# Attention opened on the in-projection's side of SBUF, beside the recurrence's last chunks

## The chip, the cores and the metric

The kernel runs on one core of a Trainium2 chip. The metric is the device time of one execution in microseconds (us). Engines: PE (TensorE matmul, with PEld its weight loads), DVE (VectorE), ACT (ScalarE), POOL (GpSimd), SP (SyncE, here the queue that issues nearly all DMAs).

## What is computed

One decoder layer over 1024 tokens of width 1024, all in float32. Cut to what matters here:

```python
h = _rmsnorm(x, mix_norm_gain)
proj = h @ w_in                                  # 1024 x 3232
p_rwkv, p_attn = proj[..., :1696], proj[..., 1696:]
y_rwkv = _rwkv7_mixer(p_rwkv, ...)               # 8 heads x 64, a recurrence over the tokens
q, k, v = split(p_attn, 3)                       # 8 heads x 64
q, k = _partial_rotary(q), _partial_rotary(k)    # first 16 of 64 dims
o = _rmsnorm(_dilated_attention(q, k, v))        # causal, three (window, dilation) patterns merged
x = x + concat([y_rwkv, o]) @ w_out
h = _rmsnorm(x); gate, val = split(h @ w_ffn_up, 2)      # 2 x 2816
x = x + (silu(_causal_dwconv(gate)) * val) @ w_ffn_down
return _rmsnorm(x)
```

## The kernel before

**A planner fixes the order.** Every step is recorded as an operation with a duration per engine that may run it, a rank (lower goes first), the operations that it waits for and the buffers that it uses. `Plan.run(until)` is a list scheduler in Python, run while the kernel is built. It takes in turn the operation that can start first by those durations, the lower rank winning, issues it, and stops once all of `until` are issued. So it writes one fixed instruction order per engine; on the chip every engine and the SP queue go through theirs strictly in order. The planner only knows waits on data and on its own rings of buffers. Where a pool is opened on the memory of a closed one, the tile framework adds waits on the chip: with `reuse_waits="tile"` the first use of a new tile waits for the last use of what lay there. SBUF and PSUM are two-ended stacks: a pool lies on the left end or, with `side="right"`, on the right end.

**The stages**, in order of time:
- The norm of x and the RWKV columns of the in-projection, with the preparation of the recurrence (prep pools, left).
- The recurrence: 16 chunks of 64 tokens in 8 units (`unit(q)`, two chunks each), pools `rp`, `pch` (the banks `pzu`, `pzs`) and `pxt` on the left, `rf` (its output side) on the right. A chunk is a chain PE L941, L950, ACT copy, PE L963, ACT copy, PE L973, L1016, DVE L989, DVE and POOL L994, to the next chunk's L941. A unit needs first a triangular solve on DVE (L869, L875), a round trip through DRAM, and two groups of small matmuls (PE L906, L912). When both chunks are done, its output is normed and stored (`yrw_d`).
- Beside it, at the lowest rank (200 + j), the twelve attention columns of the in-projection, `attn_in(j)`: 128 columns of q, k or v each, 48 matmuls of 512 columns (L456 to L458, tile `pb_at`), each half then stored to `qkv_d`. They read hT_hi and hT_lo (64 KB of each partition) and weight tiles on the right. Columns 0 to 10 may run as soon as PE has room. **Column 11 is held back** by `chain["Y"]`, the last copy of the last chunk. The rotary step (`rotated`) reloads q and k columns, turns them and stores them.
- `attention()`: per head, q and k are loaded and split in a high and a low part (ACT or DVE cast L267/L269, POOL subtractions L1149 and L1153), v is transposed (PE L1160), then for 8 blocks of queries scores (PE L1188, L1189), mask and maximum (DVE L1192), exponential (ACT L1202), transposes (PE L1220) that are split again (L1231), weighted sums (PE L1250), and two closing steps per head. Its pools (some 90 KB) are opened on the **left, over the recurrence's**, so after `left.close()`.
- The out-projection: part 0 (`y_rwkv`; PE L1383 to L1385, 192 matmuls, rank 301 and up) needs only the recurrence's output and runs beside the attention at a lower rank; part 1 needs the attention heads. Then the second norm, the FFN's up side, and its down side.

The order of these openings is written out at the end of the layer:

```python
plan.run([*rotated, *mixed_out[:-1], chain["Y"]])
left.close()
attention()
plan.run([*mixed_out, *(o for os_ in cols_out.values() for o in os_)])
right.close()
```

**PSUM** has 8 banks. Short-lived results of all stages share one ring named "t", slots in strict rotation: 4 in the recurrence (`ps` x2, `pxt` x2), 5 in the attention (`ps` x2, `pxa` x3). A slot's next user waits for its last one. `pin` (2 banks, right) belongs to the in-projection, `pzu` and `pzs` to the recurrence, `pa` (1) to the attention, `pacc` (2) to the out-projection.

Of the kernel before, what the change touches and what calls it, by code (L numbers as in the profile page):

```python
# [15 lines left out]
PSUM = bass.MemoryType.PSUM  # L16
# [53 lines left out]
class Buf:  # L70


    def __init__(self, ring, make):
        self.ring, self.make, self.t, self.ops = ring, make, None, []

    def free_at(self):
        return None if any(o.end is None for o in self.ops) else max(o.end for o in self.ops)


class Plan:  # L80
# [70 lines left out]
    def run(self, until=None):  # L151

        until = list(until) if until is not None else None
        while any(self.todo.values()):
# [3 lines left out]
            for eng, ops in self.todo.items():  # L158
# [5 lines left out]
                s, i = got[0]  # L164
# [9 lines left out]
            for b in o.bufs:  # L174
                if b.t is None:
                    b.t = b.make()
                    self.used[b.ring].append(b)
# [24 lines left out]
def planned_layer(ctx: ExitStack, tc: tile.TileContext, a, out):  # L202
# [10 lines left out]
    plan = Plan()  # L213
# [18 lines left out]
    turns = []  # L232

    def t_ring(*pools):
        turns[:] = pools
        plan.ring("t", len(pools))
        plan.banks.add("t")

    def t_new(name):
        def make():  # L240
            pool, tag = turns[len(plan.used["t"]) % len(turns)]
            return pool.tile([P, 512], F32, tag=tag, name=name)

        return plan.buf("t", make)
# [463 lines left out]
    def attn_in(j, after=None):  # L708
        R = 200 + j

        def evacuate(n, acc, m, d):
            spl = spl_n(f"spl{j}_{n}")

            def put(eng):
                if j >= 4:
                    copy(eng, spl.t, acc.t)
                else:
                    scaled(eng, spl.t, acc.t, 0.125)

# [353 lines left out]
    cols_out[11] = attn_in(11, chain["Y"])  # L1073
# [44 lines left out]
    def attention():  # L1118
        pa = att.enter_context(tc.tile_pool(name="pa", bufs=1, space=PSUM, reuse_waits="tile"))
        pxa = att.enter_context(tc.tile_pool(name="pxa", bufs=3, space=PSUM, reuse_waits="tile"))  # L1120
        ap_ = att.enter_context(tc.tile_pool(name="ap", bufs=1, reuse_waits="tile"))
        t_ring((ps, "t"), (pxa, "x"), (pxa, "x"), (ps, "t"), (pxa, "x"))
# [12 lines left out]
        def head_operands(h, R):  # L1135
# [3 lines left out]
            qin = [load(qd, lambda b=b: qd.t[b : b + 64], lambda: heads[h], 0.73, R) for b in (0, 64)]  # L1139
# [3 lines left out]
                    cols_out[8 + h // 2] if b else (),  # L1143
# [619 lines left out]
    xpool = outp.enter_context(tc.tile_pool(name="xpool", bufs=1, side="right", reuse_waits="tile"))  # L1763
    wop = outp.enter_context(tc.tile_pool(name="wop", bufs=1, side="right", reuse_waits="tile"))
    wop0 = wop0_.enter_context(tc.tile_pool(name="wop0", bufs=1, side="right", reuse_waits="tile"))
# [4 lines left out]
    low, up_left, up_right, at = ExitStack(), ExitStack(), ExitStack(), {}  # L1770
    at["low"] = low.enter_context(tc.tile_pool(name="rawp", bufs=1, reuse_waits="tile"))
    pup = up_left.enter_context(tc.tile_pool(name="pup", bufs=1, space=PSUM, reuse_waits="tile"))
    hp2 = up_left.enter_context(tc.tile_pool(name="hp2", bufs=1, reuse_waits="tile"))
    tmpn_ = ExitStack()
    pxn = tmpn_.enter_context(tc.tile_pool(name="pxn", bufs=2, space=PSUM, reuse_waits="tile"))
    tmpn = tmpn_.enter_context(tc.tile_pool(name="tmpn", bufs=1, reuse_waits="tile"))
# [14 lines left out]
    dlow = dlow_.enter_context(tc.tile_pool(name="dlow", bufs=1, side="right", reuse_waits="tile"))  # L1791
    at["ps1"] = up_right.enter_context(tc.tile_pool(name="ps1", bufs=1, space=PSUM, side="right", reuse_waits="tile"))
    at["late"] = up_right.enter_context(tc.tile_pool(name="late", bufs=1, side="right", reuse_waits="tile"))
# [5 lines left out]
    at["last"] = up_right.enter_context(tc.tile_pool(name="last", bufs=1, side="right", reuse_waits="tile"))  # L1799
    at["ps2"] = up_right.enter_context(tc.tile_pool(name="ps2", bufs=1, space=PSUM, side="right", reuse_waits="tile"))  # L1800
# [5 lines left out]
    up_right.close()  # L1806
    up_left.close()
    dn_ = ExitStack()
    pdn = dn_.enter_context(tc.tile_pool(name="pdn", bufs=6, space=PSUM, reuse_waits="tile"))
    dp = dn_.enter_context(tc.tile_pool(name="dp", bufs=1, side="right", reuse_waits="tile"))  # L1810
# [83 lines left out]
```

## Time and profile before

| | |
|---|---|
| median of 3 runs | 1441.2 us (1432.59 to 1442.34) |
| profiled execution: its own time, its span | 1448.17 us, 1446.0 us |
| PE busy over the span | 1378.2 us (95%) |
| DVE, ACT, POOL busy | 999.4, 555.0, 334.1 us |
| mean granted TensorE clock | 0.979 of full |

The rows below are times from the span's start. In the views of stretches each engine has its busy time and its count of instructions; PEclk is the mean granted clock, 1.00 standing for 2.4 GHz and 0.50 for 1.2 GHz; then the share of the 16 DMA engines and GB/s. In a timeline the columns are start, duration, engine, line, operation, output<-inputs, shapes, count, and in brackets the idle time just before and what ended it.

### The profile page before, as it was taken

What the parts mean: (1) busy time and instruction counts of PE and PEld (TensorE: products, weight loads), DVE (VectorE), ACT (ScalarE), POOL (GpSimd) and SP (SyncE); (2) the same over time, 40 slices, a digit from 0 to 9 for tenths busy, and PEclk for the clock granted to TensorE, in tenths of its full rate; (3) what the DMA queues carried; (4) which work ended last, traced back from release to release, by engine and by line L of the source; (5) the groups of instructions that cost most, each with busy time, mean ns of one, the idle gap of its engine ahead of it and who ended that gap; (6) DMA issues with size and microseconds to landing.
All of it is one profiled execution on the core that took longest, in us unless ns stands there. A gap on an engine that the chain in (4) does not pass through costs nothing.

```text
span 1446.0 us, 21020 instructions
## 1 busy us (share of the span) xinstructions
PE 1378.2 (95%) x7872; PEld 1137.7 (79%) x7872; DVE 999.4 (69%) x2018; ACT 555.0 (38%) x961; POOL 334.1 (23%) x364
## 2 busy tenths in 40 slices
PE   5999999999999889999889999999999998999997
PEld 4788887788777778898767888888888876888886
DVE  5566663878777279897678867677776757565556
ACT  5432332133332268775344434433333434122113
POOL 4223223144443367642211000000000004111101
PEclk9999999999999899999989999999999999999999
DMA  6143348545653365432633322222222228322203
GB/s 180 44 145 119 129 140 253 147 138 138 175 146 88 87 200 151 131 114 88 220 131 98 88 87 74 72 87 82 79 87 88 69 79 288 123 97 88 88 29 117
DMA packets 172564, 173.02 MB, mean 120 GB/s; under 512 B 39632, under 2 KB 142416, under 8 KB 171440
## 3 DMA queue, kind: packets, MB, share of 16 engines
q1 hardware_dynamic: 172320, 171.16, 38.9%
q8 instruction: 62, 1.02, 0.3%
q10 hardware_dynamic: 144, 0.52, 0.1%
q14 instruction: 38, 0.31, 0.1%
HBM read 119.22 MB, written 52.43 MB: 119 GB/s over the span
## 4 chain that ended last, share of the span: by engine, by line
PE 53%; DVE 4%; DMA 2%; issue 1%; ACT 1%; POOL 1%; SPq 0%; DVEq 0%; POOLq 0%; ACTq 0%
PE c L1536 29%; PE pd L1736 5%; PE pd L1734 5%; PE pd L1735 5%; PE po L1250 2%; PE ppt L1220 2%; PE po L1383 1%; PE po L1385 1%; PE po L1384 1%; PE psc L1188 1%; PE psc L1189 1%; DVE T L1480 1%; DVE T L1488 1%; DMA rw<-in_w_down 1%; DVE fjk L1711 1%
## 5 line engine op out<-in xcount | busy, mean ns | idle before, releaser
L282 POOL TENSOR_TENSOR wl<-rw,wh 128x512 fp32r<-128x512 f32 x22 | 31.5, 1435 | 565.5 <-ACT wh L1421 543.8
L1742 DVE TENSOR_TENSOR dx<-dx,pd 128x512 f32<-128x512 f32 x128 | 86.6, 686 | 87.2 <-PE pd L1736 86.4
L1736 PE MATMUL pd<-wl,ah 128*128 128x512 f32 x352 | 138.0, 392 | 2.3 <-POOL wl L282 2.3
L1735 PE MATMUL pd<-wh,al 128*128 128x512 f32 x352 | 138.0, 392 | 2.0 <-POOL al L282 2.0
L1734 PE MATMUL pd<-wh,ah 128*128 128x512 f32 x352 | 137.9, 392 | 1.0 <-DVE uval L1607 1.0
L1607 DVE TENSOR_TENSOR uval<-uval,c 128x512 f32<-128x512 f32 x67 | 45.9, 685 | 66.5 <-PE c L1536 66.3
L456 PE MATMUL pb_at<-hT_hi,wh_at 128*128 128x512 f32 x192 | 82.0, 427 | 0.0
L1736 PEld LDWEIGHTS pd<-wl,ah 128*128 128x128 f32 x352 | 66.6, 189 | 17.1 <-POOL wl L282 3.2
L1735 PEld LDWEIGHTS pd<-wh,al 128*128 128x128 f32 x352 | 66.6, 189 | 16.1 <-POOL al L282 2.4
L1734 PEld LDWEIGHTS pd<-wh,ah 128*128 128x128 f32 x352 | 66.5, 189 | 15.5 <-DVE uval L1607 1.4
L458 PE MATMUL pb_at<-hT_hi,wl_at 128*128 128x512 f32 x192 | 76.5, 399 | 0.0
L457 PE MATMUL pb_at<-hT_lo,wh_at 128*128 128x512 f32 x192 | 76.4, 398 | 0.0
L1638 DVE SCALAR_TENSOR_TENSOR uga<-ug,par,uga 128x1023 f32<-128x1023 f32 (+1 forms) x44 | 56.3, 1280 | 15.2 <-ACT uga L1632 15.2
L869 DVE TENSOR_TENSOR it<-mk,mp 128x60 f32<-128x60 f32 (+19 forms) x240 | 64.5, 286 | 3.3
L1536 PE MATMUL c<-B,a11h 128*128 128x512 f32 x176 | 56.5, 402 | 0.5 <-ACT B L1478 0.2
L1536 PE MATMUL c<-T,s1h 128*128 128x512 f32 x176 | 55.6, 396 | 0.3 <-DVE T L1480 0.3
L1202 ACT ACTIVATE sm<-sm,mx 128x128 f32<-128x128 f32 (+3 forms) x64 | 49.5, 775 | 15.9 <-DVE mx L1192 15.8
L1536 PE MATMUL c<-T,a22h 128*128 128x512 f32 x176 | 55.4, 396 | 0.0
L1536 PE MATMUL c<-T,s3h 128*128 128x512 f32 x176 | 55.3, 396 | 0.0
L1536 PE MATMUL c<-B,s4h 128*128 128x512 f32 x176 | 55.3, 396 | 0.0
L1536 PE MATMUL c<-T,s2h 128*128 128x512 f32 x176 | 55.3, 395 | 0.0
L1536 PE MATMUL c<-B,a12h 128*128 128x512 f32 x176 | 55.0, 393 | 0.0
(335 smaller groups left out, 3744.3 us busy)
## 6 DMA issues: line engine op xcount, KB each, us to landing
rg<-in_w_up SPq DMA_DIRECT2D x22, 512.0 KB
rv<-in_w_up SPq DMA_DIRECT2D x22, 512.0 KB
ra<-act_d SPq DMA_DIRECT2D x22, 512.0 KB
rw<-in_w_down SPq DMA_DIRECT2D x22, 512.0 KB
act_d<-uga SPq DMA_DIRECT2D x21, 512.0 KB
x<-in_x SPq DMA_DIRECT2D x16, 512.0 KB
wr_at<-in_w_in SPq DMA_DIRECT2D x12, 512.0 KB
qkv_d<-spl SPq DMA_DIRECT2D x24, 256.0 KB
```

The costliest lines, as they stand in the source:

```text
L456: nc.tensor.matmul(acc.t[:m, cs], hi.t[:, k, :m], hT_hi[k][:, ts_], start=(k == 0), stop=False)
L457: nc.tensor.matmul(acc.t[:m, cs], hi.t[:, k, :m], hT_lo[k][:, ts_], start=False, stop=False)
L458: nc.tensor.matmul(acc.t[:m, cs], lo.t[:, k, :m], hT_hi[k][:, ts_], start=False, stop=(k == KD - 1))
L869: nc.vector.tensor_tensor(t3(), mk.t[:, k : k + 1, k + 1 :].broadcast_to([P, r, n]), mp.t[:, 0:r, k : k + 1].broadcast_to([P, r, n]), ALU. ...
L1202: nc.scalar.activation(sm.t[:, :L], sm.t[:, :L], AF.Exp, bias=mx.t[:, x : x + 1], scale=-1.0, accum_out=den.t[:, i : i + 1])
L1536: nc.tensor.matmul(bank.t, w.t[:, js], m, start=start and j == 0 and s, stop=j == 3 and w is lo, skip_group_check=True,)
L1607: {DVE: 0.69}, lambda: nc.vector.tensor_tensor(half_of(*out_), half_of(*x_), four(bank), ALU.add), R, after,
L1638: lambda x=x: nc.vector.scalar_tensor_tensor(ga.t[:, x:], g.t[:, : S - x], pc(f"cw{2 - x}", f), ga.t[:, x:], ALU.mult, ALU.add),
L1734: nc.tensor.matmul(pd.t, ah.t[:, ts_], wh.t, start=(j == 0), stop=False)
L1735: nc.tensor.matmul(pd.t, al.t[:, ts_], wh.t, start=False, stop=False)
L1736: nc.tensor.matmul(pd.t, ah.t[:, ts_], wl.t, start=False, stop=(j == n_ - 1))
L1742: lambda i=i, sl=sl, pd=pd: nc.vector.tensor_add(xr[i].t[:, sl], xr[i].t[:, sl], pd.t), R,
```

## The change

- Column 11 is no longer held back; all twelve columns are filler beside the recurrence.
- `rf` moves from the right to the left, under `rp`, and `pxt` is opened before `pch`. Nothing of the recurrence is left on the right.
- As soon as the rotary step and all twelve columns are planned, the right side is closed and `attention()` opens there, over the in-projection's memory, while the recurrence still runs on the left. The attention's loads of q and k are made to wait for all of `rotated`.
- The two PSUM banks of `pin` become `pa` and one `pxa` bank. The ring "t" grows to 5 slots (`ps` x2, `pxt` x2, `pxa`), shared by both stages. When the last unit's output is planned, `t_less(pxt)` takes two slots away, the left side closes, `pacc` takes two of its banks and `pxb` two, and `t_more` adds the latter: again 5.
- The out-projection then opens on the left. The second norm and the start of the FFN change to the right, the rest of the FFN to the left: a mirror image of before, with the same sizes.
- Slots of "t" are now objects with a pool of their own, where before they were counted off.

Cut to its core:

```diff
+    def t_more(*pools):
+        u, n = plan.used["t"], plan.rings["t"]
+        new = [Buf("t", None) for _ in pools]
+        for b, s in zip(new, pools):
+            b.slot = s
+        u[len(u) - n : len(u) - n] = new
+        plan.rings["t"] = n + len(pools)
...
+    def t_less(pool):
+        u, n = plan.used["t"], plan.rings["t"]
+        gone = [b for b in u[len(u) - n :] if b.slot[0] is pool]
+        plan.used["t"] = [b for b in u[len(u) - n :] if b.slot[0] is not pool]
+        plan.rings["t"] = n - len(gone)
+        plan.run([o for b in gone for o in b.ops])
...
-    cols_out = {j: attn_in(j) for j in range(11)}
+    cols_out = {j: attn_in(j) for j in range(12)}
...
+    rf = left.enter_context(tc.tile_pool(name="rf", bufs=1))
     rp = left.enter_context(tc.tile_pool(name="rp", bufs=1))
+    pxt = left.enter_context(tc.tile_pool(name="pxt", bufs=2, space=PSUM))
     pch = left.enter_context(tc.tile_pool(name="pch", bufs=1, space=PSUM))
-    pxt = left.enter_context(tc.tile_pool(name="pxt", bufs=2, space=PSUM))
-    rf = right.enter_context(tc.tile_pool(name="rf", bufs=1, side="right"))
...
-    cols_out[11] = attn_in(11, chain["Y"])
...
-        pa = att.enter_context(tc.tile_pool(name="pa", bufs=1, space=PSUM, reuse_waits="tile"))
-        pxa = att.enter_context(tc.tile_pool(name="pxa", bufs=3, space=PSUM, reuse_waits="tile"))
-        ap_ = att.enter_context(tc.tile_pool(name="ap", bufs=1, reuse_waits="tile"))
-        t_ring((ps, "t"), (pxa, "x"), (pxa, "x"), (ps, "t"), (pxa, "x"))
+        pa = att.enter_context(tc.tile_pool(name="pa", bufs=1, space=PSUM, side="right", reuse_waits="tile"))
+        pxa = att.enter_context(tc.tile_pool(name="pxa", bufs=1, space=PSUM, side="right", reuse_waits="tile"))
+        ap_ = att.enter_context(tc.tile_pool(name="ap", bufs=1, side="right", reuse_waits="tile"))
+        t_more((pxa, "x"))
...
-            qin = [load(qd, lambda b=b: qd.t[b : b + 64], lambda: heads[h], 0.73, R) for b in (0, 64)]
+            qin = [load(qd, lambda b=b: qd.t[b : b + 64], lambda: heads[h], 0.73, R, rotated) for b in (0, 64)]
...
-    plan.run([*rotated, *mixed_out[:-1], chain["Y"]])
+    plan.run([*rotated, *(o for os_ in cols_out.values() for o in os_)])
+    right.close()
+    attention()
+    plan.run(mixed_out)
+    t_less(pxt)
     left.close()
-    attention()
-    plan.run([*mixed_out, *(o for os_ in cols_out.values() for o in os_)])
-    right.close()
     outp, wop0_ = ExitStack(), ExitStack()
-    pacc_ = outp.enter_context(tc.tile_pool(name="pacc", bufs=2, space=PSUM, side="right", reuse_waits="tile"))
+    pacc_ = outp.enter_context(tc.tile_pool(name="pacc", bufs=2, space=PSUM, reuse_waits="tile"))
+    pxb = att.enter_context(tc.tile_pool(name="pxb", bufs=2, space=PSUM, reuse_waits="tile"))
+    t_more((pxb, "x"), (pxb, "x"))
...
```

What is left out moves the pools of the later stages to the other side, word for word otherwise.

## Rows read from the trace of the kernel before

**Rows 1.** The page's 40 slices: PE busy and granted clock, in tenths.

```profile
PE   5999999999999889999889999999999998999997
PEclk9999999999999899999989999999999999999999
```

**Rows 2.** Busy time by stretch: PE, PEld, DVE, ACT, POOL, then PEclk, DMA.

```profile
400.00:455.00 55.00, 54.09 (x541) 43.42 (x541) 44.80 (x169) 16.13 (x27) 25.01 (x33) 1.00 0.47 119
455.00:485.00 30.00, 25.46 (x289) 22.84 (x288) 10.44 (x39) 6.36 (x11) 7.71 (x14) 0.66 0.29 72
485.00:497.00 12.00, 9.09 (x125) 8.05 (x126) 3.70 (x11) 3.55 (x7) 4.63 (x5) 1.00 0.08 25
497.00:513.00 16.00, 14.13 (x64) 11.32 (x64) 5.56 (x14) 3.98 (x6) 8.63 (x6) 0.89 0.86 230
513.00:525.00 12.00, 10.35 (x71) 8.45 (x71) 11.30 (x36) 9.97 (x24) 8.78 (x6) 1.00 0.92 288
525.00:545.00 20.00, 16.73 (x107) 14.36 (x106) 14.85 (x35) 14.10 (x31) 12.27 (x15) 0.91 0.56 150
545.00:690.00 145.00, 142.92 (x991) 127.93 (x991) 127.68 (x335) 103.09 (x221) 76.91 (x98) 1.00 0.40 121
690.00:765.00 75.00, 64.47 (x292) 52.25 (x292) 54.28 (x74) 30.43 (x57) 14.22 (x22) 0.93 0.53 174
```

**Rows 3.** Timeline of the recurrence's last chunks on PE.

```profile
458.77 1.17 PE L906 MATMUL pd<-inv,Gm 32*32 32x32 f32 x32
...
476.57 1.97 PE L963 MATMUL pzu<-zs,Gm 128*64 128x64 f32 x16
...
483.86 1.13 PE L941 MATMUL pzu<-state,AR 128*128 128x128 f32 x8 [0.72 <-POOL sp L986]
...
486.78 1.15 PE L963 MATMUL pzu<-zs,Gm 128*64 128x64 f32 x16 [0.72 <-ACT zs L267]
488.60 0.69 PE L973 MATMUL pzs<-UV,BKt 128*64 128x64 f32 x16 [0.67 <-ACT UV L267]
489.12 1.10 PE L1016 MATMUL pzu<-UV,Gm 128*64 128x64 f32 x16
```

**Rows 4.** Timeline of column 10's last matmuls and of column 11's second half.

```profile
457.06 0.39 PE L457 MATMUL pb_at<-hT_lo,wh_at 128*128 128x512 f32 x1
457.29 0.39 PE L458 MATMUL pb_at<-hT_hi,wl_at 128*128 128x512 f32 x1
...
506.77 0.48 PE L456 MATMUL pb_at<-hT_hi,wh_at 128*128 128x512 f32 x1
```

**Rows 5.** Timeline of POOL and DVE side by side in the recurrence.

```profile
444.16 2.37 POOL L282 TENSOR_TENSOR wl_at<-wr_at,wh_at 128x1024 fp32r<-128x1024 f32 x1 [2.60 <-issue]
444.21 2.50 DVE L869 TENSOR_TENSOR it<-mk,mp 128x21 f32<-128x21 f32 x2
```

**Rows 6.** Timeline of the first head's way in, on SP, ACT, POOL and PE.

```profile
496.50 0.45 SPq L285 DMA_DIRECT2D amask<-in_amask  x1
...
503.51 1.05 ACT L267 CAST q<-qd 128x1024 fp32r<-128x1024 f32 x1 [3.27 <-DMA qd<-qkv_d]
...
504.64 2.35 POOL L1149 TENSOR_TENSOR q<-qd,q 128x1024 fp32r<-128x1024 f32 x1 [0.55 <-ACT q L267]
507.06 2.37 POOL L1153 TENSOR_TENSOR k<-kv,k 64x1024 fp32r<-64x1024 f32 x1
...
505.75 0.68 PE L1160 MATMUL pav<-cst,kv 64*128 64x64 f32 x8 [1.87 <-DMA kv<-qkv_d]
...
512.59 0.23 PE L1188 MATMUL psc<-k,q 128*128 128x128 f32 x1
```

**Rows 7.** The rotary step's stores, by tile: count, durations, first and last start.

```profile
L285 SPq DMA_DIRECT2D qkv_d<-x_rot x8: 603/618/880, 286.0 to 404.9; - x8
```

**Rows 8.** Timeline: the out-projection's first matmul.

```profile
524.59 0.48 PE L1383 MATMUL po<-wo_h,yh 128*128 128x512 f32 x1
```

More of the change, by code (lines that the diff above doesn't have):

```diff
@@ L73, in __init__ @@
     def __init__(self, ring, make):
-        self.ring, self.make, self.t, self.ops = ring, make, None, []
+        self.ring, self.make, self.t, self.ops, self.slot = ring, make, None, [], None
     def free_at(self):
-        return None if any(o.end is None for o in self.ops) else max(o.end for o in self.ops)
+        return None if any(o.end is None for o in self.ops) else max((o.end for o in self.ops), default=0.0)
 class Plan:
@@ L175, in run @@
                 if b.t is None:
+                    u, n = self.used[b.ring], self.rings[b.ring]
+                    if len(u) >= n:
+                        b.slot = u[len(u) - n].slot
                     b.t = b.make()
-                    self.used[b.ring].append(b)
+                    u.append(b)
             o.fn(eng) if len(o.how) > 1 else o.fn()
@@ L230, in ring2 @@
         return new, lambda name: plan.buf(tag, lambda: pool.tile(shape, F32R, tag=tag, name=name, bufs=n))
-    turns = []
+    def t_more(*pools):
[5 more added lines that the diff above has]
+        plan.rings["t"] = n + len(pools)
     def t_ring(*pools):
-        turns[:] = pools
-        plan.ring("t", len(pools))
+        plan.ring("t", 0)
         plan.banks.add("t")
+        t_more(*pools)
+    def t_less(pool):
[4 more added lines that the diff above has]
+        plan.run([o for b in gone for o in b.ops])
     def t_new(name):
         def make():
-            pool, tag = turns[len(plan.used["t"]) % len(turns)]
+            pool, tag = b.slot
             return pool.tile([P, 512], F32, tag=tag, name=name)
-        return plan.buf("t", make)
+        b = plan.buf("t", make)
+        return b
     def pe(us):
@@ L1142, in head_operands @@
                     kv, lambda b=b: kv.t[b : b + 64], lambda b=b: heads[8 + h + b // 8], 0.73, R,
-                    cols_out[8 + h // 2] if b else (),
+                    cols_out[8 + h // 2] if b else rotated,
                 )
@@ L1769, in planned_layer @@
     att.close()
[L1770 to L1773, printed above, removed]
+    low, up_low, up_late, at = ExitStack(), ExitStack(), ExitStack(), {}
+    at["low"] = low.enter_context(tc.tile_pool(name="rawp", bufs=1, side="right", reuse_waits="tile"))
+    pup = up_low.enter_context(tc.tile_pool(name="pup", bufs=1, space=PSUM, side="right", reuse_waits="tile"))
+    hp2 = up_low.enter_context(tc.tile_pool(name="hp2", bufs=1, side="right", reuse_waits="tile"))
     tmpn_ = ExitStack()
-    pxn = tmpn_.enter_context(tc.tile_pool(name="pxn", bufs=2, space=PSUM, reuse_waits="tile"))
-    tmpn = tmpn_.enter_context(tc.tile_pool(name="tmpn", bufs=1, reuse_waits="tile"))
+    pxn = tmpn_.enter_context(tc.tile_pool(name="pxn", bufs=2, space=PSUM, side="right", reuse_waits="tile"))
+    tmpn = tmpn_.enter_context(tc.tile_pool(name="tmpn", bufs=1, side="right", reuse_waits="tile"))
     t_ring((ps, "t"), (ps, "t"), (pxn, "x"), (pxn, "x"))
@@ L1790, in planned_layer @@
     dlow_ = ExitStack()
-    dlow = dlow_.enter_context(tc.tile_pool(name="dlow", bufs=1, side="right", reuse_waits="tile"))
-    at["ps1"] = up_right.enter_context(tc.tile_pool(name="ps1", bufs=1, space=PSUM, side="right", reuse_waits="tile"))
-    at["late"] = up_right.enter_context(tc.tile_pool(name="late", bufs=1, side="right", reuse_waits="tile"))
+    dlow = dlow_.enter_context(tc.tile_pool(name="dlow", bufs=1, reuse_waits="tile"))
+    at["ps1"] = up_late.enter_context(tc.tile_pool(name="ps1", bufs=1, space=PSUM, reuse_waits="tile"))
+    at["late"] = up_late.enter_context(tc.tile_pool(name="late", bufs=1, reuse_waits="tile"))
     begin(1)
@@ L1798, in planned_layer @@
     tmpn_.close()
-    at["last"] = up_right.enter_context(tc.tile_pool(name="last", bufs=1, side="right", reuse_waits="tile"))
-    at["ps2"] = up_right.enter_context(tc.tile_pool(name="ps2", bufs=1, space=PSUM, side="right", reuse_waits="tile"))
+    at["last"] = up_late.enter_context(tc.tile_pool(name="last", bufs=1, reuse_waits="tile"))
+    at["ps2"] = up_late.enter_context(tc.tile_pool(name="ps2", bufs=1, space=PSUM, reuse_waits="tile"))
     acts += [up(f) for f in range(1, NF)]
@@ L1805, in planned_layer @@
     plan.run([*acts, *(o for e_ in early for o in e_[2])])
-    up_right.close()
-    up_left.close()
+    up_late.close()
+    up_low.close()
     dn_ = ExitStack()
     pdn = dn_.enter_context(tc.tile_pool(name="pdn", bufs=6, space=PSUM, reuse_waits="tile"))
-    dp = dn_.enter_context(tc.tile_pool(name="dp", bufs=1, side="right", reuse_waits="tile"))
+    dp = dn_.enter_context(tc.tile_pool(name="dp", bufs=1, reuse_waits="tile"))
     down(acts, early, dp, pdn)
```

6 lines of the change are left out of this document (3 added, 3 removed).

## Prediction, written before the changed kernel was run

> **What bounds the kernel now.** I read the page's slices first, then busy times by stretch, then the timeline around the two hand-overs. In the slices (36 us each) PE is at 9 almost everywhere and falls in the first, in 14 and 15 (470 to 542 us), in 20 and 21 (687 to 759), 34 and the last; its clock dips in 14 and 21 [rows 1]. By stretch this gets sharper [rows 2]: from 545 to 690, attention with the out-projection as filler, PE lacks 2.1 us of 145, so this stage is bound by PE's total work, and work put earlier comes off its end. Time can only be won where PE stands idle or runs at the lower of its two clock levels. The change touches the stretch from 455 to 545, which holds the last four chunks of the recurrence and the attention's first two heads. PE's idle time there is 4.5 + 2.9 + 1.9 + 1.7 + 3.3 = 14.2 us. The clock costs busy time x (1 - PEclk): 25.46 x 0.34 = 8.7, 14.13 x 0.11 = 1.6 and 16.73 x 0.09 = 1.5, together 11.7 us. That this loss is real shows in one matmul group of the recurrence, 1.97 us at 1.2 GHz and 1.15 us at 2.4 GHz [rows 3]. **25.9 us is thus the pool** out of which this change can pay. DVE, 88% busy from 545 to 690, is only 34% busy from 455 to 497 (14.1 of 42 us), so it has room for an early attention too.
>
> **The change, part by part.**
>
> *Column 11 as filler.* Before, the filler ends with column 10 at 457.7 [rows 4]. PE then has only the recurrence; its busy share falls and the clock goes to 1.2 GHz. Column 11 is 48 matmuls at a pitch of 0.23 us [rows 4], 11 us of PE. Will it fit beside the recurrence? A chunk's matmuls take 1.13 + 2 x 1.15 + 0.69 + 1.10 = 5.2 us at full clock, a group of the solve 1.17 [rows 3]. From 457.7 to the start of the last but one chunk at 483.9 lie one chunk without its first group (4.1), one whole chunk (5.2), four groups of the solve (4.7) and one transposed output (0.7, an estimate: as the short group L973): 14.7 us of 26.2, so 11.5 us are free. I take column 11 to end at 483. Bounds: 469 if the planner let it run through, 492 if the chain, faster at full clock, left it room only at the end. Its weights cost nothing more: the subtraction at 444.16 is the last of the twelve columns', so column 11's is made that early before as well, under column 9's and 10's matmuls [rows 5].
>
> *The attention's start.* Its memory comes free with column 11's last matmul. Behind that stand the copy and store of that column, about 1.5 us (an estimate from the 1.05 us cast and two issues of 0.45 in [rows 6]), then the same loads as before. From the first load's issue at 496.50 to the end of the second POOL subtraction, 507.06 + 2.37, it took 12.9 us [rows 6]; first scores would so come at 483 + 1.5 + 12.9 = 497, against 512.6. Before, they were kept back 3.2 us more by column 11's second half, in front of them on PE since 506.8 [rows 4, 6]; that goes too. The head start is 15 us, with the bounds of column 11 between 6 and 29 us. The DMAs per head are the same in number; on SP they stand behind column 11's store, which itself ends after the memory is free, so their new waits on memory hold up nothing of the recurrence. The new wait on `rotated` costs nothing: its last store was issued at 404.9 [rows 7], 78 us earlier.
>
> *Two stages in the same queues.* This is the wait that the change adds. In the first head ACT waits 3.27 us for q to land and PE 1.87 us for v [rows 6]. Before, the recurrence was over by then. Now ACT's copies and PE's groups of the last chunk are queued behind these, and POOL's part of the state behind two subtractions of 2.4 us. No row shows how often it happens; from nothing (the loads land in time) to all of it once per head for two heads, 2 x (3.3 + 1.9) = 10 us on the recurrence's end. I take 5. Who waits for that end? Only part 0 of the out-projection, PE's filler, which began at 524.6 [rows 8]. Without that filler PE is 86% busy (10.35 of 12), with it 98.6% [rows 2], so 5 us cost 0.6 us.
>
> *PSUM.* The attention has five slots of "t" before and after; while the recurrence shares them, and three for the moment between `t_less` and `t_more`. Nothing in the trace shows a wait for a slot as such; I take nothing, and as a bound the 1.7 us that PE idles in 513 to 525 once more, either way.
>
> *The sides.* `rf` and the mirrored later stages: nothing. They have the same sizes and the same order of opening, and from 765 on PE is full in every slice up to the seam [rows 1]. If a side does cost something, the stretch from 690 to 765, with 10.5 us of idle PE, is where it can be seen; I allow 1 us either way.
>
> *The sum*, as PE time that is still lost between 457 and 545. To 483: 1.7% idle as in 400 to 455, where filler and recurrence ran together, 0.4 us, and no loss of clock. From 483 to 497 the recurrence alone: 24% idle as in 485 to 497, 3.4 us, at full clock as there. From 497 to 525 the attention with the last of the recurrence and no filler: 513 to 545 lost 4.9 us of idle time and 1.5 of clock in 32, 20%; of 28 us that is 5.6, and 0.6 for the later filler. From 525 to 545 part 0 begins: between 1.4% and the 24% (with clock) of that stretch before; I take 10%, 2 us. Together 12 us, rounded up to 13 for what the two queues do to each other. 25.9 - 13 = **13 us faster**. The head start of 15 us, less some 2 for the shared queues, says the same. On the profiled execution, 1448.2 us, this makes 1435; on the median of the runs, which lies 7 us lower, 1441.2 - 13 = 1428.
>
> *A rule that speaks against it.* While POOL subtracted 128 x 1024 elements in 2.37 us, two small DVE operations of the solve took 2.50 us [rows 5]. The Trainium skill, "SBUF — State Buffer", section "Who interferes with whom", says that a VectorE instruction with two SBUF inputs and a GpSimd instruction that reads SBUF exclude each other for the whole instruction; this row agrees. By that rule the four such subtractions of the first two heads would each hold the state's sum of a chunk, up to 9.5 us on the recurrence's end; at the price of 0.12 us per us this takes 1.1 us from the gain, 12 in place of 13.
>
> **The rivals.**
> - *Most of the pool is won.* The planner fits column 11 in by about 470, the clock never falls, and head 0 starts at 485, where DVE and ACT are free. Then the losses are 0.4 + 4.5. 25.9 - 5 = 21 us: 1420. For it: the 34% of DVE; against: the recurrence ranks before all filler, and PE's room by 470 is only half of what column 11 needs.
> - *It doesn't begin beside the recurrence.* Column 11 ends at 492, scores start at 506, and their 14 us of loads and splits, which column 11 covered before, stand bare with one chunk beside them: about 7 us idle and 5 of clock, besides 0.6 before and 10 as in the sum after. 25.9 - 23 = 3 us: 1438. For it: the recurrence at full clock is faster (1.15 for 1.97 us), so the last chunks may be over when the memory comes free.
> - *Slower: the attention's waits for its loads stand in front of the last chunk.* Column 11 ends late as in the case above, and ACT's 3.3, PE's 1.9 and POOL's 4.7 us all fall on one chain, 10 us. PE then idles half of 20 us and goes through the ramp at 1.2 GHz, as from 455 to 485 (8.7 us), and part 0 comes 10 us later (1.2). Losses: 0.6 + 10 + 8.7 + 8 + 2 = 29 us, 3 to 4 us more than the pool: 1445. It is slower from the point where the losses pass 25.9 us. For it: [rows 6], where these very waits stand. Against: the planner knows a load's length roughly, and puts the recurrence first.
>
> **How the numbers follow.** Chances: the forecast 0.50, most of the pool 0.20, hardly any overlap 0.18, slower 0.12. The range reaches from 1416 (the second case with the bounds of PSUM and sides and a little more head start) to 1445 (the last case), and leaves some 0.2 outside. One per cent, 14.4 us, is about what a measurement of this kernel can tell from no change; the runs shown differ by 0.7%. Faster by more than that: the second case nearly whole (0.18) and the part of the forecast above 14.4 us, just over a third (0.18): 0.36. Slower by more than 1%: the tail of the last case and what I haven't thought of, 0.09. The rest, 0.55, is within 1%. So the likeliest time lies close under the bound, and the signs are less in doubt than the size.
>
> **What would show it.** Right: L456 to L458 run on without a break from 457 to about 483; PEclk stays at 1.00 there; the first L1188 comes at about 497, before or just after the last L1016; L1383 begins at 520 to 530; the stretch from 545 on looks as before, but each mark in it, and the first L1536 of the FFN, some 13 us earlier, and PE's loss between 455 and 545 is about 13 us in place of 25.9. Wrong: column 11 ending after 490, a gap of PE over 3 us between it and the first L1188 with a fall of the clock, ACT or PE waiting for qd or kv while recurrence groups are still to come, or heads that follow each other more slowly than before; and a longer stretch between attention and FFN would say that the mirrored sides matter.

## The result and the profile after

The changed kernel takes 1431.9 us (median of 16 runs, 1426.7 to 1435.8), the kernel before beside it 1440.9 (16 runs, 1432.6 to 1452.0): ratio 0.9933, interval 0.9914 to 0.9952, **9.0 us faster**. The forecast was 13 us, which is no change by the bound of 1%. A later set of runs (the yardstick below) gave 0.9912. Time, direction and range held. The reason did not: most of the 9 us does not come from the stretch that the prediction was about, but from a stage that it took to be untouched.

The profiled execution took 1431.92 us, its span is 1430.1. That of the kernel before took 1448.17 and lay 7.3 us above the median of 1440.9, so the two traces differ by more than the change is worth. I compare stages first, and check each against other runs of the same order of instructions.

The page's slices of the changed kernel, PE busy and granted clock, in tenths [rows 1]:

```profile
PE   5999999899999889999889999999999999999997
PEclk9999999999999999999989999999999999999999
```

Its busy time by stretch, columns as in [rows 2]:

```profile
455.00:485.00 30.00, 29.28 (x357) 24.00 (x356) 10.22 (x37) 8.65 (x15) 6.09 (x12) 1.00 0.30 78
485.00:497.00 12.00, 6.57 (x72) 5.92 (x69) 4.50 (x13) 3.73 (x5) 8.37 (x6) 0.86 0.88 200
497.00:513.00 16.00, 13.82 (x110) 11.48 (x110) 13.66 (x42) 12.76 (x29) 7.64 (x7) 1.00 0.41 111
513.00:525.00 12.00, 10.53 (x85) 9.47 (x84) 10.35 (x31) 8.34 (x21) 9.03 (x12) 1.00 0.37 89
525.00:545.00 20.00, 17.03 (x114) 14.33 (x113) 17.80 (x51) 15.41 (x32) 14.03 (x14) 0.91 0.77 238
```

Column 11 does what it should: from 455 to 485 PE is 98% busy at full clock, where 4.5 us were idle and 8.7 us went to the clock [rows 2]. The dip moves to 485 to 497, where PE idles 5.4 of 12 us. Idle time (0.7 + 5.4 + 2.2 + 1.5 + 3.0) and clock (6.57 x 0.14 + 17.03 x 0.09) lose 15.2 us in the 90, against 25.9 before.

The timeline of the changed kernel on PE, SP, ACT, DVE and POOL shows the hand-over (lines are 18 or 19 higher than before; answers to [rows 3, 4, 6, 8]):

```profile
480.89 0.40 PE L477 MATMUL pb_at<-hT_hi,wl_at 128*128 128x512 f32 x1
...
491.72 1.11 PE L1178 MATMUL pav<-cst,kv 64*128 64x64 f32 x8 [4.25 <-DMA kv<-qkv_d]
...
493.67 1.74 PE L960 MATMUL pzu<-state,AR 128*128 128x128 f32 x8
...
498.23 0.33 PE L1206 MATMUL psc<-k,q 128*128 128x128 f32 x1
...
499.23 1.15 PE L1035 MATMUL pzu<-UV,Gm 128*64 128x64 f32 x16
...
545.26 0.45 PE L1401 MATMUL po<-wo_h,yh 128*128 128x512 f32 x1
...
515.81 1.08 SPq L304 DMA_DIRECT2D qd<-qkv_d  x2
516.94 0.59 SPq L304 DMA_DIRECT2D yb<-bon_d  x1
...
524.46 0.36 SPq L304 DMA_DIRECT2D yrw_d<-yb  x1
...
489.28 1.04 ACT L286 CAST q<-qd 128x1024 fp32r<-128x1024 f32 x1 [3.48 <-DMA qd<-qkv_d]
...
506.30 0.67 DVE L1054 TENSOR_REDUCE stat<-Y 128x8 f32<-128x512 f32 x1
...
513.39 2.39 POOL L1167 TENSOR_TENSOR q<-qd,q 128x1024 fp32r<-128x1024 f32 x1
515.74 1.05 POOL L1062 TENSOR_TENSOR Y<-Y,stat 128x512 f32<-128x512 f32 x1
...
541.98 1.29 POOL L301 TENSOR_TENSOR yl<-yr,yh 128x512 fp32r<-128x512 f32 x1
```

Column 11 ends at 481 (forecast 483), the first scores stand at 498.2 (forecast 497; 512.6 before [rows 6]): a head start of 14.4 us. A part of it lies ahead of the stretch. Chunk 12 of the recurrence, counted from 0 to 15, starts with this group in the kernel before and in the changed one:

```profile
450.38 1.14 PE L941 MATMUL pzu<-state,AR 128*128 128x128 f32 x8
```

```profile
448.03 1.05 PE L960 MATMUL pzu<-state,AR 128*128 128x128 f32 x8
```

Executions differ by that much there without the change too (table below), so I also count from the start of chunk 12. By that count the head start is 12.0 us (62.2 before, 50.2 after).

But PE waits 4.25 us for head 0's v with chunk 15 queued behind it, and **part 0 of the out-projection begins at 545.3, 20.7 us later than before** [rows 8], 23 us counted from chunk 12.

Then the stages behind it. The last matmul of the out-projection and the last product of the FFN's up side, in the kernel before (count, durations in ns, first and last start):

```profile
L1385 PE MATMUL po<-wo_l,yh x128: 387/392/628, 525.1 to 752.3; 128*128 128x512 f32 x128
...
L1536 PE MATMUL c<-T,a22h x176: 393/394/472, 782.7 to 1189.4; 128*128 128x512 f32 x176
```

and in the changed one:

```profile
L1403 PE MATMUL po<-wo_l,yh x128: 387/390/629, 545.8 to 744.9; 128*128 128x512 f32 x128
...
L1554 PE MATMUL c<-T,a22h x176: 389/393/472, 774.8 to 1174.5; 128*128 128x512 f32 x176
```

The out-projection ends 7.4 us earlier, 5.0 counted from chunk 12. From there to the end of the up side it was 1189.4 - 752.3 = 437.1 us and is 429.6: **7.5 us in a stage that the prediction said would not change**. PE is full in it in both kernels, so its busy share says nothing. The count of matmuls does. Kernel before:

```profile
800.00:900.00 100.00, 100.00 (x431) 1.00 0.28 85
900.00:1000.00 100.00, 100.00 (x432) 1.00 0.27 81
```

Changed kernel:

```profile
800.00:900.00 100.00, 100.00 (x440) 1.00 0.28 85
900.00:1000.00 100.00, 100.00 (x439) 1.00 0.27 81
```

The same 128x512 matmuls follow each other every 232 ns before and every 227.5 ns after, both at 2.4 GHz. That became the main question.

### The profile page after: what moved, and what is told of

Same layout as the page of the kernel before. It is cut to its first block, busy times and chain, and to the rows that moved or that the text cites. A ratio compares the mean times of both kernels' runs of the same rounds, so it can differ in the third digit from the quotient of the medians.

```text
span 1430.1 us, 20997 instructions
## 1 busy us (share of the span) xinstructions
PE 1368.6 (96%) x7872; PEld 1134.4 (79%) x7872; DVE 999.6 (70%) x2023; ACT 555.6 (39%) x959; POOL 331.7 (23%) x361
## 4 chain that ended last, share of the span: by engine, by line
PE 76%; DVE 12%; DMA 6%; ACT 2%; issue 1%; SPq 1%; POOL 1%; DVEq 0%; POOLq 0%; ACTq 0%
PE c L1554 28%; PE pd L1754 5%; PE pd L1752 5%; PE pd L1753 5%; PE po L1268 2%; PE pb_at L475 2%; PE ppt L1238 2%; PE pb_at L477 2%; PE pb_at L476 2%; PE po L1401 1%; DVE it L888 1%; PE po L1402 1%; PE po L1403 1%; DVE mp L894 1%; SPq L304 1%
## 5 line engine op out<-in xcount | busy, mean ns | idle before, releaser
L301 POOL TENSOR_TENSOR wl<-rw,wh 128x512 fp32r<-128x512 f32 x22 | 31.7, 1444 | 558.7 <-ACT wh L1439 535.5
L1752 PEld LDWEIGHTS pd<-wh,ah 128*128 128x128 f32 x352 | 66.8, 190 | 14.4 <-DVE dx L288 0.4
L1656 DVE SCALAR_TENSOR_TENSOR uga<-ug,par,uga 128x1023 f32<-128x1023 f32 (+1 forms) x44 | 56.3, 1280 | 15.2 <-ACT uga L1650 15.2
L888 DVE TENSOR_TENSOR it<-mk,mp 128x60 f32<-128x60 f32 (+19 forms) x240 | 60.6, 270 | 3.3
L894 DVE TENSOR_TENSOR mp<-mp,it 128x60 f32<-128x60 f32 (+20 forms) x240 | 55.8, 249 | 3.4
```

Source lines behind the costliest of these rows:

```text
L888: nc.vector.tensor_tensor(t3(), mk.t[:, k : k + 1, k + 1 :].broadcast_to([P, r, n]), mp.t[:, 0:r, k : k + 1].broadcast_to([P, r, n]), ALU. ...
L894: nc.vector.tensor_tensor(mp.t[:, 0:r, k + 1 :], mp.t[:, 0:r, k + 1 :], t3(), ALU.add)
L1656: lambda x=x: nc.vector.scalar_tensor_tensor(ga.t[:, x:], g.t[:, : S - x], pc(f"cw{2 - x}", f), ga.t[:, x:], ALU.mult, ALU.add),
L1752: nc.tensor.matmul(pd.t, ah.t[:, ts_], wh.t, start=(j == 0), stop=False)
```

## The experiments

Two theories to start with. A: the gain is PE time won back around the recurrence's end, and the late part 0 ate the rest of it. B: it is something else that came with the change. Stages by trace (starts in us; "up" is from the out-projection's last matmul to the up side's last with a22h, both as in the lines above, "rest" from there to the end of the span; "lost" is PE's idle time and clock from 455 to 545) and ratios by runs. The ratios' own spread is some 0.2 to 0.3%, 3 to 4 us; the up side repeats within 0.5 us:

| kernel | chunk 12 | first scores | part 0 | out-proj. ends | lost | up | rest | ratio to before |
|---|---|---|---|---|---|---|---|---|
| before | 450.4 | 512.6 | 524.6 | 752.3 | 26.0 | 437.1 | 256.6 | 1 |
| column 11 free | 450.3 | 509.3 | 525.4 | 749.1 | 22.3 | 437.0 | 257.5 | 0.9995 |
| no overlap | 446.5 | 506.0 | 523.4 | 747.9 | 24.9 | 429.5 | 253.1 | 0.9910 |
| changed | 448.0 | 498.2 | 545.3 | 744.9 | 15.2 | 429.6 | 255.6 | 0.9933 |
| changed, again | 448.1 | 498.5 | 546.5 | 745.8 | 16.3 | 429.6 | 253.6 | 0.9912 |
| before + pad | 449.4 | 517.5 | 529.5 | 757.9 | 33.1 | 426.0 | 256.6 | 0.9952 |
| column 11 free + pad | 446.0 | 504.2 | 521.4 | 746.2 | 24.0 | 426.0 | 256.6 | 0.9914 |
| no overlap + pad | 447.9 | 507.1 | 523.6 | 747.9 | 23.0 | 426.5 | 251.8 | 0.9887 |
| changed + pad | 447.2 | 498.6 | 546.6 | 746.1 | 17.7 | 426.0 | 253.6 | 0.9899 |
| v later | 444.7 | 492.2 | 530.4 | 742.7 | 15.8 | 429.6 | 250.3 | 0.9936 |
| truer figures | 448.9 | 496.6 | 530.8 | 740.0 | 12.2 | 429.4 | 252.9 | 0.9842 |
| truer figures + pad | 448.6 | 496.2 | 531.2 | 741.3 | 13.6 | 426.1 | 252.7 | 0.9851 |
| early loads | 451.0 | 498.6 | 534.1 | 746.9 | 15.6 | 426.0 | 254.0 | 0.9868 |

Each line is one execution. They do not reach chunk 12 at the same time: column 11 free with and without the pad, whose order is the same, differ by 4.3 us there. So marks up to the out-projection's end are better compared as distances from chunk 12. Three of the executions are far from the median of their kernel: before (7.3 us above it), before + pad (5.7 above) and v later (10.5 below); the others lie within 2.5 us.

**Column 11 free**, in the kernel before:

```
-    cols_out = {j: attn_in(j) for j in range(11)}
+    cols_out = {j: attn_in(j) for j in range(12)}
...
-    cols_out[11] = attn_in(11, chain["Y"])
```

> The kernel before, with column 11 as plain filler like columns 0 to 10 and nothing else changed: the attention still opens on the recurrence's side, after the last chunk. Theory A (the early filler alone pays little: it removes the 13 us that PE lost from 455 to 485, but takes the same work out of the 16 us from 497 to 513, where it hid the way in of the first head): first scores come 2 to 4 us earlier than in the kernel before, and the time is 3 us shorter, about 1438. Theory B (by stretches, 12.5 of the 10.7 us that the change won net lie before 485, so the filler is the whole gain and the overlap gives nothing): 9 us shorter, about 1432.

Measured 1444.8 against 1444.2 us, 0.9995 (0.9974 to 1.0015). Theory A's 3 us are seen in the trace (first scores 3.3, the out-projection's end 3.2 us earlier), not in the median; B in the form "the filler is the whole gain" is out. From 497 to 513 PE is now busy for 4.8 of 16 us, so the filler only moved:

```profile
497.00:513.00 16.00, 4.84 (x20) 3.63 (x20) 6.14 (x20) 4.59 (x7) 8.65 (x7) 0.57 0.90 208
```

**No overlap**, in the changed kernel (the same for q, k and v):

```
-        mask_in = load(amask, ..., 1.0, 90)
+        mask_in = load(amask, ..., 1.0, 90, [chain["Y"]])
```

> The changed kernel with the attention's first loads (mask, q, k, v) made to wait for the last copy of the last chunk: column 11 as filler, all pools on their new sides, the PSUM ring grown and shrunk, but no overlap. If the new sides cost nothing, it comes within 2 us of the kernel before with column 11 free, and by theory A at 3 us below the kernel before, about 1438. If the mirrored sides or the ring cost something, it is slower than that one by more than 2 us. By theory B (the overlap gives nothing) it keeps the changed kernel's time, 1432.

Measured 1431.1 us, 0.9910 (0.9882 to 0.9938): as fast as the changed kernel, although PE loses as much around the recurrence's end as in the kernel before. Its stretches:

```profile
455.00:485.00 30.00, 28.61 (x369) 23.51 (x368) 9.44 (x35) 8.64 (x15) 6.81 (x12) 1.00 0.27 73
485.00:497.00 12.00, 6.14 (x80) 5.30 (x76) 4.56 (x13) 2.95 (x5) 3.89 (x5) 0.93 0.43 117
497.00:513.00 16.00, 7.78 (x32) 5.91 (x33) 6.74 (x24) 6.42 (x14) 10.18 (x8) 0.50 0.85 222
513.00:525.00 12.00, 11.32 (x62) 10.02 (x62) 9.03 (x25) 7.53 (x15) 6.00 (x3) 0.74 0.97 264
525.00:545.00 20.00, 18.50 (x133) 16.07 (x132) 16.63 (x46) 16.98 (x37) 15.04 (x16) 1.00 0.49 123
```

16 us at 1.2 GHz and half idle cost nothing that the median shows. Against column 11 alone it is 12 us better, and the table says where: 7.5 us in the up side, 4.4 behind it, 1.2 before it. So **the sides, priced at nothing, are worth more than the overlap** (this run does not part them from the PSUM ring, which changed with them). Part of theory A fell here; B now needed a mechanism.

**Start addresses.** In the built programs the FFN's moving operands (the tiles T and B) start at byte 416 of a kilobyte before and 992 after, and the stationary ones (s1 to s4, a22) the other way round, since the left end of SBUF begins with tiles of odd sizes. The exception are a11 and a12 of every other block, which lie on the moving operands' side. In the kernel before they alternate (trace: a12 227.7 and 233.5 ns, block by block), while s1 to s4 always take 233 to 234. No trace shows an address; the alternation pointed to the starts. One pad makes all of them 992:

```
     half = cp.tile([P, 16], F32, name="half")
+    pad = cp.tile([P, 144], F32, name="pad")
+    nc.gpsimd.memset(pad, 0.0)
```

The third of these expectations names the mark of the table for the up side, but its 420.8 and 413.6 us begin some 16 us later, near the first product with s1. The difference is 7.2 us by those figures and 7.5 by the table's.

> The kernel before with 576 bytes of each partition added at the bottom of SBUF's left end (one tile that is set to zero and never read), and nothing else: order and sides stay. In the FFN's up side the moving operands lie on the left, from byte 416 of a kilobyte on, the weights mostly on the right, from byte 992 on; the pad brings both to 992. Theory C (what makes these matmuls 233 ns apart in the kernel before and 229 in the changed one is where the two operands start, and alike starts are best): pitch 226 to 228 ns, FFN up side 413 us or less, 7 us shorter, 0.995. Theory D (it is the side itself, or the distance of the two operands): pitch stays at 233, time unchanged, 1.000.

> The changed kernel with the same pad of 576 bytes at the bottom of the left end. Here the moving operands of the FFN's up side lie on the right from byte 992 on and most weights on the left from byte 416 on; with the pad both start at 992. Theory C: the pitch falls from 229 to 226 or 227 ns in all products, the up side gets 2 to 4 us shorter, ratio to the changed kernel 0.998. Theory D: pitch and time as in the changed kernel.

> The changed kernel once more, unaltered, as the yardstick for the runs beside it and for a second profile. Ratio to the kernel before 0.993; FFN up side (from the last matmul of the out-projection's yh to the last of the up side) 413.6 us as in the first profile, against 420.8 in the kernel before, if the faster matmuls of that stage belong to the kernel and not to one execution.

Theory C held in every stage it named. The up side is 426.0 us with the pad in both kernels, and 429.6 again in the repeat. The kernel before with the pad:

```profile
800.00:900.00 100.00, 100.00 (x442) 1.00 0.29 85
900.00:1000.00 100.00, 100.00 (x443) 1.00 0.28 83
```

In time: before with the pad 1437.1 us, 0.9952 (0.9923 to 0.9981); changed with the pad 1427.5, 0.9899 (0.9874 to 0.9924); changed again 1431.5, 0.9912 (0.9879 to 0.9945). The first of these gains 7 us where its up side shows 11.1. Its runs spread from 1426.5 us to over 1446, and its profiled one had a bad passage elsewhere:

```profile
455.00:485.00 30.00, 25.59 (x284) 23.14 (x282) 9.78 (x36) 6.36 (x11) 7.29 (x13) 0.60 0.27 63
485.00:497.00 12.00, 9.89 (x83) 9.03 (x83) 1.53 (x3) 2.27 (x4) 4.01 (x5) 0.50 0.08 24
```

The order of instructions is that of [rows 2], but the clock stays at 1.2 GHz to 497 instead of coming back before 485, and the first scores come 4.9 us later. So two executions of one order, with and without the pad, differ by 7 us in this stretch alone. The pad need not be the reason: runs of the padded kernel itself had mean granted clocks from 0.970 (1446.6 us) to 0.986 (1426.5 us).

**The law by itself.** 32 matmuls per group, only the start bytes change:

```
nc.tensor.matmul(c, w[:, o : o + P], m[:, mo : mo + 512], ...)   # o = wo + (i % 4) * P
```

> No layer is computed: 128x512 fp32r matmuls alone, in groups of 32 on the same two tiles, after 240 to get the clock up; only the byte at which the stationary and the moving operand start changes from group to group (17 distances on neighbouring tiles, both shifted together, the moving one shifted, and a moving tile on the other end of SBUF). The output is a copy of one group's result. Theory C (starts that are alike give the shortest spacing): groups with both operands from the same byte of a kilobyte take 32 x 0.2267 = 7.25 us, those with 416 for the moving and 992 for the stationary operand 32 x 0.2333 = 7.47 us, 992 and 416 32 x 0.229 = 7.33 us, on the same side as on the other. Theory D (it is the side or the distance in SBUF, and the pad only moved something else): all groups on neighbouring tiles alike, those on the far tile slower.

Timeline of that kernel. The tile's name gives the shift of the moving and of the stationary operand in bytes (letters a to j for digits 0 to 9); without shift both start at byte 128 of a kilobyte, the tile "far" at 992. A group's time is the next start less its own:

```profile
62.10 7.42 PE L92 MATMUL n_a_a<-near,w 128*128 128x512 f32 x32
69.36 7.62 PE L92 MATMUL n_a_dc<-near,w 128*128 128x512 f32 x32
76.82 7.63 PE L92 MATMUL n_a_ge<-near,w 128*128 128x512 f32 x32
84.29 7.64 PE L92 MATMUL n_a_jg<-near,w 128*128 128x512 f32 x32
91.77 7.58 PE L92 MATMUL n_a_bci<-near,w 128*128 128x512 f32 x32
99.19 7.49 PE L92 MATMUL n_a_bjc<-near,w 128*128 128x512 f32 x32
106.52 7.43 PE L92 MATMUL n_a_cfg<-near,w 128*128 128x512 f32 x32
113.79 7.63 PE L92 MATMUL n_a_dca<-near,w 128*128 128x512 f32 x32
...
290.69 7.64 PE L92 MATMUL f_a_a<-far,w 128*128 128x512 f32 x32
298.17 7.46 PE L92 MATMUL f_a_jg<-far,w 128*128 128x512 f32 x32
305.47 7.49 PE L92 MATMUL f_a_cii<-far,w 128*128 128x512 f32 x32
312.79 7.44 PE L92 MATMUL f_a_dfc<-far,w 128*128 128x512 f32 x32
```

Shift 0 takes 7.26 us, 32, 64 and 96 take 7.46 to 7.48, 128 takes 7.42, 192 takes 7.33, 256 takes 7.27 and 320 7.47: it repeats every 256 bytes. Of the 41 groups with a successor, the 17 whose two starts differ by a multiple of 256 take 7.25 to 7.31 us (227 ns each), on either side of SBUF; five at 128 take 7.42 to 7.46; 13 at 32, 64, 96, 160 or 224 take 7.46 to 7.48. At 192 five take 7.32 to 7.34, the sixth 7.47; I have no reason for that one. The layer fits: before, 992 - 416 = 576, 64 past a multiple, 233.3 ns; after, 416 - 992, 192 past one, 228.9 ns (here f_a_cii, 305.47 to 312.79, 7.32 us); with the pad 0, 226.7 ns. Side and distance are out: theory D falls.

**The sides and the overlap with the spacing alike.** The pad in the two kernels of the first experiments:

> Column 11 as plain filler in the kernel before, with the pad of 576 bytes: matmul spacing of the FFN as in the kernel before with the pad. If the filler alone is worth nothing, as without the pad, 0.995 like that one; if it is worth the 12.5 us that PE gets back from 455 to 485, 0.987.

> The changed kernel without the overlap (first loads behind the last chunk's copy), with the pad: against the changed kernel with the pad (0.990) it differs by the overlap alone, with the spacing the same. If the overlap gives the 3 us by which the out-projection ends earlier in the profiles, 0.992; if nothing, 0.990. Against column 11 as plain filler with the pad it differs by the sides and the PSUM ring alone: if spacing was all that the sides gave, both are alike within 0.002.

Measured 1431.7 us, 0.9914 (0.9892 to 0.9935), and 1428.4 us, 0.9887 (0.9865 to 0.9910). The pad in column 11 free: 0.9995 to 0.9914, 11.7 us, where its up side shows 11.0. The overlap: 0.9887 without it, 0.9899 with it, so again no gain; by the intervals one of up to some 3 us cannot be excluded. The filler: 0.9952 to 0.9914, where without the pad it gave nothing; 0 to 5.5 us is all that I can say. The sides beyond spacing: 0.9914 to 0.9887, a little more than the 0.002 of the expectation, within the spread. But "rest" is 256.6 to 257.5 in all four executions with the old sides and 250.3 to 255.6 in all nine with the new. The seam between up and down side, 1165 to 1235, goes with it: PE is busy there for 64.3 to 64.7 us in the four and for 67.1 to 68.2 in the nine. The matmuls of the down side follow at 227 ns in all of them; what differs most is how long PE waits for the low parts of its operands (L282 and L301 are the same helper). Before:

```profile
1217.47 0.80 PE L1735 MATMUL pd<-wh,al 128*128 128x512 f32 x1 [2.04 <-POOL al L282]
1220.37 0.79 PE L1736 MATMUL pd<-wl,ah 128*128 128x512 f32 x1 [2.10 <-POOL wl L282]
```

Changed, the only such wait:

```profile
1202.29 0.80 PE L1754 MATMUL pd<-wl,ah 128*128 128x512 f32 x1 [2.84 <-POOL wl L301]
```

Why POOL comes earlier there was not tried.

**Where the overlap's head start goes.** Two edits of the changed kernel: the first records head 0's v transpose behind the last chunk, the second only gives the planner longer, truer durations for the first loads.

```
-            o = plan.op(pe(0.6), turn_v, R, [vin], [kv, pt, vhl])
+            o = plan.op(pe(0.6), turn_v, R, [vin] if h else [vin, chain["Y"]], [kv, pt, vhl])
```

> The changed kernel with head 0's v transpose recorded behind the last chunk's copy, so that it is not queued on PE in front of chunk 15. Theory A: PE no longer stands 4.25 us in front of chunk 15, the clock doesn't fall at 490 to 495, the last chunk ends 3 to 4 us earlier, and part 0 of the out-projection begins at least 4 us earlier; 2 to 4 us shorter than the changed kernel, about 1429. Rival: the way in of the first head sets the pace anyway (q and k have to land and be split before the first scores), the stall only fills a time in which nothing else could run: within 1 us of the changed kernel, 1431 to 1433.

```
-        mask_in = load(amask, ..., 1.0, 90)
+        mask_in = load(amask, ..., 2.6, 90)
-            qin = [load(qd, ..., 0.73, R, rotated) ...]          # the same for k and v
+            qin = [load(qd, ..., 0.73 if h else 1.3, R, rotated) ...]
```

> The changed kernel with only the planner's figures changed for the mask (1.0 to 2.6 us) and head 0's four loads (0.73 to 1.3 us each), near what the trace shows; the same instructions in another order: v transpose behind chunk 15's groups, and unit 7's norm on DVE ahead of the first heads' steps. Theory A (the late part 0 is what eats the rest of the gain: 20.7 us later than in the kernel before): the last chunk's output is stored 7 to 10 us earlier, part 0 begins 10 us or more earlier, 4 to 6 us shorter than the changed kernel, about 1427. Rival (part 0's start matters at 0.12 us per us, as the prediction had it): 1 to 2 us from the order of part 0, and with the wait in front of chunk 15 at most 3 us, 1429 to 1431.

> The changed kernel with the planner's figures for the mask and head 0's loads near what the trace shows, and the pad. The figures alone gave 0.984 in five runs. Theory A (the order around the last chunk and the later start of part 0 eat most of what the overlap could give): 0.984 again, less 0.002 if the pad helps, so 0.982, some 16 us below the changed kernel's neighbour run at most and at least 8. If those five runs were only a lucky draw: within 3 us of the changed kernel, 0.991 to 0.993.

The first took the wait away (chunk 15 starts at 486.1, first scores at 492.2, part 0 at 530.4) and gained nothing in the median: 1435.0 us, 0.9936 (0.9912 to 0.9960), though its runs reach from 1424.4 to 1440.2. Its profile is of the fastest of them, and even there the out-projection ends 298.0 us after chunk 12, where the changed kernel has 296.9 and 297.7. The second gives 0.9842 (0.9810 to 0.9874), with the pad 0.9851 (0.9825 to 0.9877), 1420.7 us: the two fastest of all, 10 to 13 us below the changed kernel without the pad and 7 with it. Its out-projection ends 4.9 us earlier than the changed kernel's, 5.8 counted from chunk 12. Theory A expected 4 to 6 us of the second, which gave 7 to 13, and 2 to 4 of the first, which gave none. Both have part 0 at 530 to 531 (85.6 and 81.9 us behind chunk 12, where the changed kernel has 97.2) and no wait for v in front of chunk 15, so neither of these makes the difference alone. In the second the heads take less time (first to last scores 156.5 us, 160.0 in the changed kernel, 165.2 in the first edit). What in the order does that I have not separated. Nor were the truer figures run without the overlap, so these 7 to 13 us may be the overlap's, paying at last, or the order's own.

**Early loads**, on top of the last kernel: the mask behind head 0's q, k and v, and the bonus tile of each unit as soon as its buffer is free.

```
-        mask_in = load(amask, ..., 2.6, 90)
+        mask_in = load(amask, ..., 2.6, 97)
...
-            load(b, ..., 0.8, RF, [o])
+            load(b, ..., 0.8, RF, [ys[0]] if b is yb else [o])
```

> The changed kernel with the truer figures and the pad (0.985), and two loads put earlier: the mask behind head 0's q, k and v in place of before them, and each unit's bonus tile as soon as its buffer is free in place of behind its norm. If the first scores wait for q, k and v behind the mask's 512 KB, they come 2 us earlier and part 0 of the out-projection some 4 us earlier: 0.982 to 0.983. If the POOL subtractions and the planner's order set the pace: 0.985.

Measured 1426.4 us, 0.9868 (0.9841 to 0.9895). First scores came 2.4 us later, but so did chunk 12: from there it is 47.7 us, and 47.6 without this edit, so the way in got no shorter. Part 0 came at 534.1, as far behind chunk 12 as without the edit within 1 us. The heads behind are slower (first to last scores 165.7 us, 157.3 without the edit), in another order. It gains nothing and is not kept.

## Why the prediction was near, and wrong in its reason

- **Column 11 as filler** and **the attention's start**: right in the trace. 481 for 483, 498.2 for 497, full clock to 485, PE's loss 15.2 us for 13. Counted from chunk 12 the head start is 12.0 us in place of 15.
- **"The sides: nothing", 1 us either way: this step failed.** They are worth 7.5 us in the FFN's up side, by the start bytes of the matmuls' operands, and perhaps 1 to 4 behind it, where PE waits less for POOL. I looked for their effect in the stretch from 690 to 765, where it isn't, and left out the up side since PE is full there [rows 1]. Full is not fast: PE reads 100% busy at 431 and at 440 matmuls.
- **The sum failed too, in its exchange rate.** It took each us that PE wins between 457 and 545 as a us off the end. No overlap against overlap wins 9.7 us of PE's loss (24.9 to 15.2), 5.3 with the pad; the out-projection ends 3.0 and 1.8 us earlier (4.6 and 1.2 counted from chunk 12), and no difference shows in the medians. From 545 to 690 PE is as full as before (1.4 us idle, 2.1 in [rows 2]), so a lost us does not show as idle time later; but how fast the heads follow each other changes with the planner's order (first to last scores 158.8 us without overlap, 160.0 with it), and the sum had no term for that. Where the rest of the difference goes stays open.
- **"Only part 0 waits for the recurrence's end", 5 us at 0.12**: the end came 3.5 us later (last L1035 at 499.23, before L1016 at 495.70), 5.9 counted from chunk 12, so the 5 us were well sized. But part 0 came 20.7 us later. I followed the wait on the chunk, not what stands behind it. Unit 7's first norm step on DVE stands behind the heads' steps from 501.0 (the end of the last copy) to 506.3, where before it followed at once. On POOL its scaling (L1062, 515.74) stands behind head 2's subtraction (L1167, 513.39), and the bonus load can only follow that (516.94). Its output is stored at 524.46, before at 513.86. Then yl, the low part that part 0 needs, waits on POOL behind the heads until 541.98, before until 522.80. What 20 us of later filler cost was not isolated.
- **Two stages in the same queues**: the waits I named are there, PE 4.25 and ACT 3.48 us, and stand in front of chunk 15 as the slower rival had it. That rival's price of 10 us was too high: chunk 15 starts 2.7 us later than before (490.98), 5.0 counted from chunk 12. Without these waits, in truer figures, it starts as far behind chunk 12 as before (40.3 and 40.6 us).
- **The rule of the Trainium skill on VectorE and GpSimd** that the prediction cites had nothing to act on in the recurrence's last sums: head 0's subtractions ran at 490.45 and 492.88, after the last sum of the state on DVE (488.19). The planner sees to that itself as far as its durations are right: besides the waits named ahead of the prediction, `Plan` holds POOL's operations and DVE's on SBUF apart (`port`).
- **"The case doesn't begin beside the recurrence", 3 us**, is out as a course of events, but its time is about what filler and overlap alone are worth.
- **The signs of being wrong**: two came, a gap of over 3 us on PE with a fall of the clock before the first scores, and waits for qd and kv ahead of recurrence groups. The heads follow each other 2.4 us more slowly, a third. The sign for the sides looked at the stretch between attention and FFN; the effect was in the FFN.

The forecast came out near by luck: a gain that I had not seen stood in for most of the one that I had.

## What to carry to other kernels

Before pricing a change of memory layout at nothing, count matmuls per 100 us in the stages that are full of PE, and compare the start addresses of both operands; a pad of a few hundred bytes may be worth more than a new schedule (here 3 to 11 us in the up side). A stage moved beside another brings its loads' waits into every queue of the other, so follow the last consumer (here a unit's norm and stores, then the filler) and not only the wait. Where a planner writes the order, its figures for the first loads are part of the change: truer ones, in the kernel with the overlap, won 7 to 13 us where the overlap with the old figures won nothing that shows in the medians.

## What the runs showed of the hardware

- 128x512 fp32r matmuls with a new 128x128 stationary operand each follow at 227 ns when the two operands' start bytes are equal modulo 256, and at 229 to 234 ns otherwise, at 2.4 GHz. The Trainium skill, "SBUF — State Buffer", section "Who interferes with whom", gives TensorE two independent read ports, one for the moving operand and one for weight loads, and says that PE never waits on anyone. Taken as it stands, that would give all groups the same time; they take 7.25 to 7.48 us with nothing else running, and the measurement decides. Why the starts matter is not shown.
- In a stretch of small matmuls the time at 1.2 GHz differs between executions of one order: from 485 to 497 the granted clock was 1.00 in the kernel before and 0.50 in the same with the pad, and PE lost 26.0 and 33.1 us from 455 to 545. Beside each other, the runs of the kernel before reached over 19.4 us, those of the changed one over 9.1. That such a stretch is what widens the spread is not shown: v later had the full clock from 455 to 513 and its runs reached over 15.7 us.
